# The opening stage of a two-layer hybrid decoder trunk: the scaled x in PSUM, and scalar operands in place of one-column tensors

## The chip, the cores and the metric

The kernel runs on one core of a Trainium2 chip. The metric is device time in microseconds (us) for one execution; the figure for a kernel is the median of its runs. A profile is one more execution, taken with the hardware profiler; its span goes from the first instruction to the last.

The engines are named as in the profile: PE is TensorE (matrix products; PEld is its weight load), DVE is VectorE, ACT is ScalarE, POOL is GpSimd and SP is SyncE, which here issues DMA transfers. SBUF is the on-chip memory for tiles, PSUM the smaller one (eight banks) into which PE writes its products. DVE and ACT can read and write both.

## The reference

x has 512 positions of width 1024, c is one conditioning vector of width 1024, and there are two layers:

```python
sc = jax.nn.silu(c)
for layer in range(DEPTH):
    ...
    mod = sc @ w_mod[layer] + b_mod[layer]
    shift1, scale1, gate1, shift2, scale2, gate2 = [m[:, None, :] for m in jnp.split(mod, 6, axis=-1)]

    h = rmsnorm(x, g_attn[layer]) * (1.0 + scale1) + shift1
    o = mixer_layer(h, w_in[layer], w_out[layer], diff_lambda[layer], subln_g[layer],
                    forget_bias[layer], lam_init, cos_a, sin_a, cos_b, sin_b)
    x = x + gate1 * o

    h = rmsnorm(x, g_mlp[layer]) * (1.0 + scale2) + shift2
    up = h @ w_up[layer]
    ...
    x = x + gate2 * ((jax.nn.silu(g) * u) @ w_down[layer])
return rmsnorm(x, g_final)
```

`mixer_layer` is one input projection, three kinds of attention heads and an output projection. The change touches only how the first h of layer 0 is made: the columns of `mod` for shift1 and scale1, and the line that forms h.

## The kernel before

**Layout.** x lies transposed in SBUF, as eight tiles k of 128 features by 512 positions. Every float32 operand of a large product is split in two: a rounded part hi (hh, whi) and the rest lo (hl, wlo). A product is then three matmuls, hi by hi, lo by hi and hi by lo (lines L251, L252, L253). A weight tile is loaded by DMA into raww, rounded by ACT (L174), and the rest is formed by DVE (L186).

**The opening stage (first 52 us).** c is spread over the partitions by a small product and passed through SiLU; the result stays in two PSUM tiles, cps, of 512 columns each, and also in SBUF as scb. The weight rows of w_mod for shift1 and scale1 come in as sixteen transfers of 512 KB: mu[m] holds, for the 128 features of column m, the rows of scale1 (j = 1) and of shift1 (j = 0). While they arrive, the squares of x are summed by PE into ps0, and rstd, the reciprocal root of the mean square, is made from it by ACT (L288, L289) in a PSUM tile.

Then, for each column m from 0 to 7, `unit(m)` computes the two entries of `mod`, and `attn_init` forms h and multiplies it by the first q and k weights. An entry is a dot product of a row of mu with scb. It is made in one of two ways:

- on DVE, as two products with running sum (L1043, halves of 512, mu from SBUF and cps from PSUM);
- on POOL, for the eight columns of the list POOL_COLS (shift1 of columns 1 to 7, and scale1 of column 6): POOL multiplies mu by scb (L1036, both in SBUF), ACT sums the products (L1037), and DVE adds the bias bm (L1038).

After scale1 of column m, DVE forms `scl = (1 + scale1) * g_attn` (L1046). `h_part` then does three things: DVE writes ht = x * scl * rstd (L297); ACT writes hh, which is ht + shift1 rounded (L299); DVE writes hl = (ht + shift1) - hh (L300). PE then does six matmuls, three each for q and k (L251 to L253, into the PSUM tiles qkps). After column 7 come the split of the V weights (L174, L186) and the V projection (L404 to L406), then the attention of layer 0.

**Order and buffers.** The program is written as one sequence; a planner then sets the order on each engine, places semaphores, and gives tiles their buffers. Each engine works through its own list in order. A tile pool has a fixed number of buffers for each tag, and a new tile waits until an old one is released by its last reader. ht comes from the pool tp (SBUF, tag "e", four buffers). The PSUM banks are divided into mm (three), ps_s (two), ps_t with tag "pt" (two) and ps_o (one). In the opening, the two cps hold two of the mm banks until the last L1043, ps0 holds one pt bank until rstd is formed, qkps hold both ps_s banks, and rstd holds ps_o until the last L297. The first V projection takes its four PSUM tiles from ps_o, ps_t, mm and ps_t.

`h_part` also serves all later norms (with halves of 256 columns), from other callers; those call it without the new argument.

Of the kernel before, what the change touches and what calls it, by code (L numbers as in the profile page):

```python
# [8 lines left out]
F32 = mybir.dt.float32  # L9
F32R = mybir.dt.float32r  # L10
AF = mybir.ActivationFunctionType
ALU = mybir.AluOpType
AX = mybir.AxisListType

SEQ = 512
# [15 lines left out]
def kernel(  # L31
# [27 lines left out]
    V, A, T, G = nc.vector, nc.scalar, nc.tensor, nc.gpsimd  # L59
# [10 lines left out]
    mm = ctx.enter_context(tc.tile_pool(name="mm", bufs=3, space=PS))  # L70
    ps_s = ctx.enter_context(tc.tile_pool(name="ps_s", bufs=2, space=PS))
    ps_t = ctx.enter_context(tc.tile_pool(name="ps_t", bufs=2, space=PS))
    ps_o = ctx.enter_context(tc.tile_pool(name="ps_o", bufs=1, space=PS))

    def tmp(name, tag):
        if tag == "rp":
            return rpp[0].tile([128, SEQ], F32, tag=tag, name=name, bufs=4)
        return tp.tile([128, SEQ], F32, tag=tag, name=name, bufs=4)
# [6 lines left out]
    def tick():  # L85
        for g in list(aux):
            if next(g, StopIteration) is StopIteration:
                aux.remove(g)
# [13 lines left out]
    gA = const.tile([128, DEPTH, KC], F32, name="gA")  # L102
# [8 lines left out]
    modc = const.tile([128, DEPTH, 48], F32, name="modc")  # L111
    scl = const.tile([128, DEPTH, 2, KC], F32, name="scl")
# [156 lines left out]
    ALL = slice(0, SEQ)  # L269
# [18 lines left out]
            A.activation(out=r[:, c], in_=ps[:, c], func=AF.Ln, bias=eps[:, 0:1], scale=1.0 / DM)  # L288
        A.activation(out=r[:, c], in_=r[:, c], func=AF.Exp, scale=-0.5)  # L289

    def h_part(h, l, which, k, r, c=ALL):
        if len(h) == k:
            h.append(pair_tiles(hs, "hs", "h"))
        hi, lo = h[k]
        t = tmp("ht", "e")
        sh = modc[:, l, 24 * which + k:24 * which + k + 1]
        V.scalar_tensor_tensor(out=t[:, c], in0=x[:, k, c], scalar=scl[:, l, which, k:k + 1], in1=r[:, c],  # L297
                               op0=ALU.mult, op1=ALU.mult)
        anchor[1] = A.activation(out=hi[:, c], in_=t[:, c], func=AF.Identity, bias=sh, scale=1.0).ins  # L299
        anchor[0] = V.scalar_tensor_tensor(out=lo[:, c], in0=t[:, c], scalar=sh, in1=hi[:, c].bitcast(F32),  # L300
                                           op0=ALU.add, op1=ALU.subtract).ins
# [22 lines left out]
    def attn_init(l, unit=None, ps0=None, nst=None):  # L324
        st = Init()
        h, r = nst or ([], ps_o.tile([128, SEQ], F32, tag="o", name="rstd"))
        st.h = h
        n0 = len(h)
        st.qps = [ps_s.tile([128, SEQ], F32, tag="s", name="qkps") for _ in range(2)]
        ws = []  # L330

        def q_part(k, c):
            first, last = k == 0, k == KC - 1
            for j in range(2):
                mm3(st.qps[j], ws[j](128 * k, 128 * k + 128), h[k], first, last, c)

        for half, c in enumerate(HALVES if unit is None else (ALL,)):
            if half or nst is None:
                rstd_part(r, c, ps0)
            for k in range(KC):  # L340
                if unit is not None:
                    unit(k)
                if half or k >= n0:
                    h_part(h, l, 0, k, r, c)
                if not ws:
                    ws += [W.use() for _ in range(2)]
                q_part(k, c)
                if half == 1 and k in (1, 3, 5):
                    W.pump(k // 2)
        return st  # L350
# [633 lines left out]
    with ExitStack():  # L984
        V.memset(ones, 1.0)
        V.memset(eps[:, 0:1], 1e-6)
        V.memset(eps[:, 1:2], 1e-5)
        for t, a in ((bm, bmod), (gA, gattn)):
            G.dma_start(out=t, in_=a)
        ropes = ExitStack()  # L990
        ropep[0] = ropes.enter_context(tc.tile_pool(name="rope0", bufs=1))
        with tc.tile_pool(name="start", bufs=1) as stp:
            W.pt = stp
            scp = []
            crow = [tmp("crow", "e") for _ in range(2)]
            for q in range(2):
                nc.sync.dma_start(out=crow[q][0:1, :], in_=cT[:, 512 * q:512 * q + 512])
            for q in range(2):
                cps = mm.tile([128, SEQ], F32, tag="mm", name="cps")
                T.matmul(cps, ones[0:1, :], crow[q][0:1, :], start=True, stop=True)  # L1000
                A.activation(out=scb[:, 512 * q:512 * q + 512], in_=cps, func=AF.Silu)
                last_silu[0] = A.activation(out=cps, in_=cps, func=AF.Silu).ins
                scp.append(cps)
            mus = {}
            last_load = [None]
            def mu_load(u):
                mus[u] = stp.tile([128, 2, 1024], F32, tag="mu", name="mu", bufs=6)
                for j in (1, 0):
                    src = wmod[0, 8 * j + u]
                    last_load[0] = nc.sync.dma_start(out=mus[u][:, j, :], in_=src).ins  # L1010

            for op in STARTUP:
                if op[0] == "m":
                    mu_load(int(op[1]))
                elif op == "w":
                    W.dma(W.nd + 1)
                else:
                    k = int(op[1])
                    nc.sync.dma_start(out=x[:, k:k + 2, :], in_=xT[:, k:k + 2, :])
            ps0 = ps_t.tile([128, SEQ], F32, tag="pt", name="ssps")  # L1020
            for k in range(KC):
                sq = tmp("sq", "ev")
                A.activation(out=sq, in_=x[:, k, :], func=AF.Square)
                if k % 2 == 0:
                    sq0 = sq
                    continue
                V.tensor_tensor(out=sq, in0=sq, in1=sq0, op=ALU.add)
                T.matmul(ps0, ones, sq, start=(k == 1), stop=(k == KC - 1))
            W.lo(2)

            def unit(m):
                for j in (1, 0):
                    ci = 8 * j + m
                    mu, dst, bias = mus[m][:, j, :], modc[:, 0, ci:ci + 1], bm[:, 0, ci:ci + 1]
                    if (m, j) in POOL_COLS:
                        G.tensor_tensor(out=mu, in0=mu, in1=scb, op=ALU.mult)  # L1036
                        A.activation(out=mu, in_=mu, func=AF.Copy, accum_out=dst)  # L1037
                        V.tensor_tensor(out=dst, in0=dst, in1=bias, op=ALU.add)  # L1038
                    else:
                        mp = sm.tile([128, 1], F32, tag="mp", name="mp")  # L1040
                        for q in range(2):
                            mq = mu[:, 512 * q:512 * q + 512]
                            V.tensor_tensor_reduce(out=mq, in0=mq, in1=scp[q], scale=1.0, scalar=mp if q else bias,  # L1043
                                                   op0=ALU.mult, op1=ALU.add, accum_out=dst if q else mp)
                    if j == 1:
                        V.scalar_tensor_tensor(out=scl[:, 0, 0, m:m + 1], in0=modc[:, 0, ci:ci + 1], scalar=1.0,  # L1046
                                               in1=gA[:, 0, m:m + 1], op0=ALU.add, op1=ALU.mult)

            rt0 = load_rope(ORDER[0][0])
            st = attn_init(0, unit, ps0)  # L1050
            W.pt = None
            with tc.issue_after(last_load[0]):
                for t, a in ((fb, fbias), (cst, consts), (sg, sublng), (gM, gmlp), (gF, gfin), (cw, convw),
                             (cb, convb)):
                    nc.sync.dma_start(out=t, in_=a)
        for l in range(DEPTH):
            if l:
                ropep[0] = ropes.enter_context(tc.tile_pool(name="rope%d" % l, bufs=1))
            with ropes, tc.tile_pool(name="attn%d" % l, bufs=8) as ap:
                rpp[0] = ap  # L1060
                W.pt = ap
                if l:
                    st = attn_init(l, nst=nst)
                    rt0 = load_rope(ORDER[0][0])
                nst = layer_attn(l, ap, [(0, u) for u in range(16, 40)] if l == 0 else [], st, rt0)
            with tc.tile_pool(name="mlp%d" % l, bufs=34) as mp:
                while any(g.__name__ == "mod_gen" for g in aux):
                    tick()
                anchor[0] = gate[0]
                if l == 0:  # L1070
                    aux.append(mod_gen([(0, u) for u in range(40, 48)] + [(1, u) for u in range(48)], 200))
                nst = layer_mlp(l, mp, nst)
                while aux:
                    tick()
# [106 lines left out]
```

## Time and profile before

| | us |
|---|---|
| median of three runs | 1338.02 |
| lowest and highest of them | 1337.93, 1339.64 |
| the profiled execution | 1334.63 |
| its span | 1332.9 |
| busy: PE, DVE, ACT, POOL | 1277.8, 858.2, 642.3, 22.9 |

The mean granted clock of PE is 0.989 of full speed over the span. The profile has a page of totals and shares, and views that can be asked for one stretch: what each engine waited for (a row names the waiting engine and line, the releasing one, the sum of the waits in us, how many, and the longest), instructions in order of time (start, duration, engine, line, what it writes and reads; in brackets the idle time before it), groups of instructions of one line and shape (count, sum of busy time in us and mean in ns, then the idle time before them and who ended it), and tables of busy time by stretch. Almost all of POOL's 22.9 us lies in the first 38 us.

### The profile page before, as it was taken

How to read it: one execution, taken by the hardware profiler on the slowest of the kernel's cores; microseconds unless marked ns; L12 is line 12 of the kernel's file. 1: busy time of each engine (PE TensorE's matmuls, PEld its weight loads, DVE VectorE, ACT ScalarE, POOL GpSimd, SP SyncE). 2: the span in 40 equal slices, each digit the busy share in tenths (PEclk: the TensorE clock that was granted, in tenths of full speed). 3: DMA queues.
4: the chain of work that ended last, by engine and by line, in shares of the span. 5: the costliest groups of instructions: out<-in, count | busy, mean ns of one | idle time of the engine just before them, and what ended most of it. 6: DMA issues, size and time to landing. Idle time of an engine off the chain costs nothing.

```text
span 1332.9 us, 17722 instructions
## 1 busy us (share of the span) xinstructions
PE 1277.8 (96%) x6568; PEld 1058.6 (79%) x6568; DVE 858.2 (64%) x1600; ACT 642.3 (48%) x1158; POOL 22.9 (2%) x16
## 2 busy tenths in 40 slices
PE   4899999999999999999999999999999999999997
PEld 1788888788877778888898888878878888888886
DVE  6888999868888874423347788875754444443232
ACT  5576677745333243322336677785543333333231
POOL 5100000000000000000000000000000000000000
PEclk8899999999999999999999999999999999999999
DMA  9345454433888853332432334212133333332331
GB/s 373 140 141 183 152 180 136 130 110 129 269 261 266 267 173 95 91 103 87 117 110 95 90 103 141 66 56 90 48 109 96 97 95 95 95 91 87 103 99 63
DMA packets 56601, 174.39 MB, mean 131 GB/s; under 512 B 8130, under 2 KB 10450, under 8 KB 56516
## 3 DMA queue, kind: packets, MB, share of 16 engines
q1 hardware_dynamic: 55364, 172.16, 41.0%
q8 instruction: 52, 0.85, 0.3%
q10 hardware_dynamic: 1088, 1.05, 0.2%
q14 instruction: 33, 0.27, 0.1%
q0 software_dynamic: 64, 0.06, 0.0%
HBM read 159.41 MB, written 2.10 MB: 121 GB/s over the span
## 4 chain that ended last, share of the span: by engine, by line
PE 53%; DMA 8%; DVE 7%; ACT 4%; issue 3%; SPq 0%; DVEq 0%; ACTq 0%
DMA rawm<-in_wmod_dram 7%; PE dps L251 6%; PE dps L253 6%; PE dps L252 6%; PE pu L251 4%; PE pu L253 4%; PE pu L252 4%; PE pg L252 4%; PE pg L253 4%; PE pg L251 4%; DVE wlo L186 1%; DVE rawm L217 1%; PE qkps L251 1%; PE qkps L252 1%; PE qkps L253 1%
## 5 line engine op out<-in xcount | busy, mean ns | idle before, releaser
L186 DVE TENSOR_TENSOR wlo<-raww,whi 128x1024 fp32r<-128x1024 f32 (+3 forms) x188 | 224.2, 1193 | 241.0 <-ACT whi L174 236.5
L174 ACT ACTIVATE whi<-raww 128x1024 fp32r<-128x1024 f32 (+3 forms) x188 | 194.5, 1035 | 329.6 <-PE dps L252 137.7
L253 PE MATMUL pu<-hh,wlo 128*128 128x512 f32 (+1 forms) x368 | 141.2, 384 | 3.5 <-DVE wlo L186 3.5
L252 PE MATMUL pg<-hl,whi 128*128 128x512 f32 (+1 forms) x368 | 143.0, 389 | 1.5 <-DVE hl L300 1.5
L251 PE MATMUL pg<-hh,whi 128*128 128x512 f32 (+1 forms) x368 | 141.6, 385 | 1.6 <-ACT whi L174 1.6
L251 PE MATMUL pu<-hh,whi 128*128 128x512 f32 (+1 forms) x368 | 142.4, 387 | 0.5 <-ACT whi L174 0.5
L253 PE MATMUL pg<-hh,wlo 128*128 128x512 f32 (+1 forms) x368 | 140.9, 383 | 1.1 <-DVE wlo L186 1.1
L252 PE MATMUL pu<-hl,whi 128*128 128x512 f32 (+1 forms) x368 | 140.7, 382 | 0.0
L251 PE MATMUL dps<-mh,whi 128*128 128x512 f32 x308 | 121.5, 395 | 0.0
L253 PE MATMUL dps<-mh,wlo 128*128 128x512 f32 x308 | 121.5, 394 | 0.0
L252 PE MATMUL dps<-ml,whi 128*128 128x512 f32 x308 | 121.2, 393 | 0.0
L217 DVE CUSTOM_DVE_ANT_0 rawm<-rawm,scb,bm 128x1024 f32<-128x1024 f32 x80 | 102.3, 1279 | 23.7 <-DMA rawm<-in_wmod_dram 23.4
L654 ACT ACTIVATE e<-e,nm 128x256 f32<-128x256 f32 (+3 forms) x160 | 89.0, 557 | 33.0 <-DVE nm L641 29.9
L251 PE MATMUL qkps<-hh,whi 128*128 128x512 f32 x224 | 95.1, 424 | 4.7 <-ACT qk L434 4.1
L898 ACT ACTIVATE y<-y 128x512 f32<-128x512 f32 x44 | 27.8, 632 | 142.6 <-DVE y L895 142.6
L252 PE MATMUL qkps<-hl,whi 128*128 128x512 f32 x224 | 89.7, 400 | 0.0
L253 PE MATMUL qkps<-hh,wlo 128*128 128x512 f32 x224 | 89.6, 400 | 0.0
L253 PEld LDWEIGHTS pu<-hh,wlo 128*128 128x128 f32 x368 | 69.1, 188 | 22.1 <-DVE wlo L186 6.9
L641 DVE CUSTOM_DVE_ANT_0 e<-s,cst 128x256 f32<-128x256 f32 (+3 forms) x160 | 76.4, 481 | 12.0 <-PE s L628 3.7
L252 PEld LDWEIGHTS pg<-hl,whi 128*128 128x128 f32 x368 | 69.0, 188 | 17.7 <-DVE hl L300 3.1
L253 PEld LDWEIGHTS pg<-hh,wlo 128*128 128x128 f32 x368 | 69.0, 188 | 16.7 <-DVE wlo L186 1.9
L251 PEld LDWEIGHTS pg<-hh,whi 128*128 128x128 f32 x368 | 69.1, 188 | 16.0 <-ACT whi L174 2.0
(176 smaller groups left out, 2663.2 us busy)
## 6 DMA issues: line engine op xcount, KB each, us to landing
raww<-in_wup_dram SPq DMA_DIRECT2D x88, 512.0 KB
rawm<-in_wmod_dram SPq DMA_DIRECT2D x80, 512.0 KB
raww<-in_wqk_dram SPq DMA_DIRECT2D x32, 512.0 KB
raww<-in_wdown_dram SPq DMA_DIRECT2D x32, 512.0 KB
mu<-in_wmod_dram SPq DMA_DIRECT2D x16, 512.0 KB
raww<-in_wout_dram SPq DMA_DIRECT2D x16, 448.0 KB
raww<-in_wv_dram SPq DMA_DIRECT2D x12, 512.0 KB
raww<-in_wdown_dram SPq DMA_DIRECT2D x16, 384.0 KB
```

Source lines behind the costliest of these rows:

```text
L174: A.activation(out=h[:, 0:m], in_=self.raw[i][:, c:c + m], func=AF.Copy)
L186: V.tensor_tensor(out=lo[:, 0:m], in0=raw[:, c:c + m], in1=h[:, 0:m].bitcast(F32), op=ALU.subtract)
L217: V.tensor_tensor_reduce(out=raw, in0=raw, in1=scb, scale=1.0, scalar=bm[:, l, ci:ci + 1], op0=ALU.mult, op1=ALU.add, accum_out=dst)
L251: T.matmul(ps[:, c], w[0], rhs[0][:, c], start=first, stop=False, skip_group_check=True)
L252: T.matmul(ps[:, c], w[0], rhs[1][:, c], start=False, stop=False, skip_group_check=True)
L253: T.matmul(ps[:, c], w[1], rhs[0][:, c], start=False, stop=last, skip_group_check=True)
L641: anchor[0] = V.tensor_tensor_reduce(out=e[:, 0:n], in0=s[:, 0:n], in1=cst[:, mask + SEQ - n:mask + SEQ], scale=-scale, scalar=3e38, op0=A ...
L654: anchor[1] = A.activation(out=e[:, 0:n], in_=e[:, 0:n], func=AF.Exp, bias=nm, scale=-1.0, accum_out=den).ins
L898: last_silu[0] = A.activation(out=y, in_=y, func=AF.Silu).ins
```

## The change

Three edits, all in the opening of layer 0. ht is written to PSUM there, in an mm bank for even k and a pt bank for odd k. The addition of the bias to a column summed by ACT (L1038) becomes a tensor_scalar whose scalar is read per partition. The same is done with the formation of scl (L1046).

```diff
-    def h_part(h, l, which, k, r, c=ALL):
+    def h_part(h, l, which, k, r, c=ALL, ps=False):
...
-        t = tmp("ht", "e")
+        t = (mm, ps_t)[k % 2].tile([128, SEQ], F32, tag=("mm", "pt")[k % 2], name="ht") if ps else tmp("ht", "e")
...
-                    h_part(h, l, 0, k, r, c)
+                    h_part(h, l, 0, k, r, c, ps=unit is not None)
...
-                        V.tensor_tensor(out=dst, in0=dst, in1=bias, op=ALU.add)
+                        V.tensor_scalar(out=dst, in0=dst, scalar1=bias, scalar2=None, op0=ALU.add)
...
-                        V.scalar_tensor_tensor(out=scl[:, 0, 0, m:m + 1], in0=modc[:, 0, ci:ci + 1], scalar=1.0,
-                                               in1=gA[:, 0, m:m + 1], op0=ALU.add, op1=ALU.mult)
+                        V.tensor_scalar(out=scl[:, 0, 0, m:m + 1], in0=modc[:, 0, ci:ci + 1], scalar1=1.0,
+                                        scalar2=gA[:, 0, m:m + 1], op0=ALU.add, op1=ALU.mult)
```

`unit` is given only in the opening of layer 0, so `ps` is true only there. The dot products, the shift, the splits and the matmuls are the same as before, and no transfer is added or removed.

## The prediction, made before the changed kernel was run

> **What bounds the kernel now.** I read the page first (busy time by engine, the chain that ended last), then what TensorE (PE) waited for in the whole run, longest first.
>
> ```profile
> PE 1277.8 (96%) x6568; PEld 1058.6 (79%) x6568; DVE 858.2 (64%) x1600; ACT 642.3 (48%) x1158; POOL 22.9 (2%) x16
> PE 53%; DMA 8%; DVE 7%; ACT 4%; issue 3%; SPq 0%; DVEq 0%; ACTq 0%
> ```
> ```profile
> PE ssps L1028 <- DVE sq L1027: 8.6, 1, 8.6
> PE qkps L251 <- ACT hh L299: 6.6, 3, 4.8
> PE qkps L252 <- DVE hl L300: 6.3, 3, 2.6
> PE qkps L251 <- ACT qk L434: 4.1, 2, 2.1
> PE pu L253 <- DVE wlo L186: 3.5, 7, 0.8
> ```
>
> PE is busy 96% of the span and leads the chain, so a change pays only if PE starts its work earlier or idles less. Its largest idle sums, rows one to three, are all in the opening stage, where h is made (L297 to L300) and the first q and k columns are multiplied (L251 to L253); L300 and L299 are lines that the change touches. Behind the opening no sum is above 4.1 us. Next the stretches of the opening; the columns are stretch, its length, busy time (and instructions) of PE, weight loads, DVE, ACT, POOL, then PE's granted clock, DMA share and GB/s.
>
> ```profile
> 23.00:52.24 29.24, 18.60 (x49) 12.05 (x49) 27.93 (x51) 14.71 (x24) 15.32 (x7) 0.65 0.52 200
> 33.19:36.61 3.42, 2.98 (x7) 2.16 (x7) 3.42 (x8) 1.76 (x3) 3.42 (x2) 0.52 1.05 402
> 36.61:40.02 3.41, 1.42 (x5) 0.67 (x4) 3.41 (x6) 0.00 (x0) 1.71 (x2) 0.99 0.31 80
> 40.02:43.43 3.41, 2.55 (x6) 1.97 (x7) 3.37 (x12) 2.89 (x5) 0.00 (x0) 0.50 0.01 2
> 43.43:46.85 3.42, 3.42 (x8) 2.21 (x8) 3.35 (x8) 2.75 (x6) 0.00 (x0) 0.52 0.00 0
> 46.85:50.26 3.41, 2.74 (x12) 1.88 (x10) 2.57 (x8) 1.92 (x4) 0.00 (x0) 1.00 0.00 0
> 52.00:64.00 12.00, 12.00 (x99) 11.94 (x98) 7.54 (x12) 4.22 (x7) 0.00 (x0) 1.00 0.55 205
> ```
>
> From 23.00 to 52.24 DVE is busy 27.93 of 29.24 us: **DVE bounds the opening**. From 52.24, when the V projection starts, PE is busy without a gap. The DMA share falls to 0.31 in the third row and to nothing after it, so the opening's loads are in by about 38 us and do not set its end. The timelines of DVE, POOL and PE (start, us, what) show where DVE's time goes.
>
> ```profile
> 25.97 2.52 DVE L300 SCALAR_TENSOR_TENSOR hl<-ht,modc,hh 128x512 fp32r<-128x512 f32 x1
> 28.41 2.32 DVE L1046 SCALAR_TENSOR_TENSOR scl<-modc,gA 128x1 f32<-128x1 f32 x1
> ...
> 31.39 2.17 DVE L300 SCALAR_TENSOR_TENSOR hl<-ht,modc,hh 128x512 fp32r<-128x512 f32 x1
> 33.49 0.74 DVE L297 SCALAR_TENSOR_TENSOR ht<-x,scl,rstd 128x512 f32<-128x512 f32 x1
> 34.15 0.74 DVE L1043 CUSTOM_DVE_ANT_0 mu<-mu,cps,mp 128x512 f32<-128x512 f32 x1
> 34.81 0.08 DVE L1043 DVE_READ_ACCUMULATOR2_ANT modc<- 128x1 f32 x1
> 34.81 1.01 DVE L1038 TENSOR_TENSOR modc<-modc,bm 128x1 f32<-128x1 f32 x1
> ...
> 36.41 2.26 DVE L300 SCALAR_TENSOR_TENSOR hl<-ht,modc,hh 128x512 fp32r<-128x512 f32 x1
> 38.60 0.15 DVE L1046 SCALAR_TENSOR_TENSOR scl<-modc,gA 128x1 f32<-128x1 f32 x1
> ...
> 50.41 0.75 DVE L300 SCALAR_TENSOR_TENSOR hl<-ht,modc,hh 128x512 fp32r<-128x512 f32 x1 [0.79 <-ACT hh L299]
> ```
> ```profile
> 19.48 18.65 POOL L1036 TENSOR_TENSOR mu<-mu,scb 128x1024 f32<-128x1024 f32 x7 [7.83 <-DMA mu<-in_wmod_dram]
> ```
>
> The same L300 takes 2.17 to 2.52 us while POOL multiplies (19.48 to 38.07 us) and 0.75 us afterwards; the 128x1 operations take 2.32 and 1.01 us in place of 0.15. What suffers has its tensor inputs in SBUF. What has one of two in PSUM does not: L297 (rstd in PSUM) and L1043 (cps in PSUM) keep 0.74 us at 33.49 and 34.15, in the midst of POOL's work. The wait hangs on two inputs from SBUF.
>
> **The change, part by part.** *ht in PSUM.* L300 then reads one tensor from PSUM, as L297 and L1043 do. Three of the eight L300 fall in POOL's time: 2.52 + 2.17 + 2.26 - 3 x 0.75 = 4.70 us less. *L1046 and L1038 as tensor_scalar.* One of each waits inside DVE's busy stretch: 2.32 - 0.15 = 2.17 and 1.01 - 0.15 = 0.86, together 3.03 us. Sum on DVE: **7.73 us**. (The two weight splits of L186 at 18.89 us, also slow, stay as they are.) The prices of the new forms, from the groups by line and shape:
>
> ```profile
> L312 DVE SCALAR_TENSOR_TENSOR x<-dps,modc,x 128x512 f32<-128x512 f32 x14 | 10.5, 750 | 30.6 <-PE dps L253 30.6
> L669 DVE SCALAR_TENSOR_TENSOR e<-e,rd 128x512 f32<-128x512 f32 x8 | 6.0, 746 | 0.1
> L356 DVE TENSOR_SCALAR sg<-sg 128x1 f32<-128x1 f32 x2 | 0.3, 146 | 0.0
> L1001 ACT ACTIVATE scb<-cps 128x512 f32<-128x512 f32 x2 | 1.2, 597 | 3.0 <-PE cps L1000 3.0
> L1002 ACT ACTIVATE cps<-cps 128x512 f32<-128x512 f32 x2 | 1.2, 592 | 0.0
> ```
>
> A PSUM input costs DVE 750 against 746 ns, a tensor_scalar 146 ns against 0.15 us. No row shows DVE writing PSUM; ACT writes PSUM in 592 against 597 ns to SBUF. By these rows eight ht tiles cost between -0.04 and +0.03 us: nothing. L299 reading PSUM on ACT is priced the same way, and ACT has slack (14.71 of 29.24 us).
>
> *Waits added.* Two of the three mm banks hold cps until the last L1043, so the even ht share one bank: ht of column k+2 must wait for L300 of column k. In DVE's own order it stands behind that L300 already (ht of column 2, at 33.49, behind L300 of columns 0 and 1), so this costs nothing; without that order it would be one L300, 0.75 us, per even column, with DVE's column products behind it. The odd ht alternate between two pt banks once rstd is computed. The V projection's banks now wait for the last ht, but its first matmul stands on PE behind the L252 of column 7, which needs the same L300: nothing added. The change adds no DMA, and no instruction passes a queue.
>
> *What is late next.* Taking DVE's order as it is, without the waits, an L300 ends where it ended less the waits ahead of it and its own: column 0 at 26.7 us (25.97 + 0.75), column 1 at 28.2 (31.39 + 0.75 - 1.77 - 2.17), column 2 at 31.0 (less 1.42 and 0.86 more), column 7 at 43.4 (50.41 + 0.75 - 7.73). ACT, half idle, keeps up with its hh and its sums of POOL's products, and POOL still ends by 38 us, ahead of column 7. PE may not keep up, because of its clock:
>
> ```profile
> 45.23 0.63 PE L253 MATMUL qkps<-hh,wv 128*128 128x512 f32 x1
> 45.66 0.63 PE L252 MATMUL qkps<-hl,wv 128*128 128x512 f32 x1
> ...
> 47.33 0.40 PE L253 MATMUL qkps<-hh,wv 128*128 128x512 f32 x1
> 47.56 0.40 PE L252 MATMUL qkps<-hl,wv 128*128 128x512 f32 x1
> ```
>
> Start to start a matmul takes 0.43 us at granted clock 0.5 and 0.23 at 1.0. At half clock throughout, the 46 matmuls behind the first L300 take 46 x 0.43 = 19.8 us from 26.7: PE ends at 46.5 in place of 52.24, a gain of 5.7. At full clock for the last columns DVE sets the end and the gain is 7.7. The clock rows say which is nearer: it rose after a stretch in which PE was busy 2.98 of 3.42 us, and again after 3.42 of 3.42; it fell after 1.42 of 3.41. In the new order the first three columns keep PE at work from 26.7 us for (18 - 2) x 0.43 = 6.9 us, to 33.6, without a gap (each L300 above is early enough), twice such a stretch, so the rise comes before column 4. I take **7.2 us**, half a microsecond below the upper end for a possible fall of the clock between the later columns. Nothing behind 52.24 starts at a fixed time, so the whole gain reaches the end. Against the profiled execution (1334.63 us, span 1332.9) that is 1327.4 us. The median of the three runs is 1338.02, 3.4 us above it; I predict against the median: 1338.02 - 7.2 = **1330.8 us**.
>
> *The skill against the second edit.* The rows above show waits only for two SBUF tensors. The Trainium skill (SBUF — State Buffer, Who interferes with whom) counts tensor_scalar among the operations that can enter a two-port mode and then take the same port pair as GpSimd. [...]
>
> **The rivals.** *PE at half clock throughout* (worked out above): gain 5.7, 1332.3 us. Against it speaks the rise after busy stretches; for it, that the clock stayed at 0.50 through 40.02 to 43.43 with PE busy 2.55 of 3.41.
>
> *The small operations still wait.* L300 gains its 4.70, but tensor_scalar waits for POOL as the old forms did. With DVE ahead, some five of them in separate places fall before 38 us; at half a POOL product each (18.65/7/2 = 1.3 us, and some overlap) they take about 5.5 us in place of 3.03: gain 2.2, 1335.8 us. For it: no row excludes it. Against: the one tensor input of such an operation leaves nothing for a second read.
>
> *The change doesn't do what it says*: L300 waits with ht in PSUM too. Gain at most the 3.03 us of the small ones, 1335.0, and more likely under 2, about 1337. L297 and L1043 speak against it.
>
> *Slower: the order behind the opening.* The order on each engine is planned from costs; new operands in the opening can turn choices in layer 0's attention, where DVE is nearly full. The price is that of a wait which is there now:
>
> ```profile
> 140.00:150.00 10.00, 7.89 (x38) 6.82 (x38) 8.62 (x23) 5.89 (x16) 0.00 (x0) 0.83 0.38 106
> ```
>
> PE idles 10.00 - 7.89 = 2.1 us, on a q or k split (L434, longest wait 2.1 us above), and a mean clock of 0.83 over 10 us is 3.4 us at half clock, which cost 1.7 us of work: 3.8 us together. One new such wait leaves a gain of 3.4, two make it nothing (1338.4), three give 1330.8 + 11.4 = **1342.2 us**: from the third on this decides. Against it: no instruction behind the opening changes.
>
> **How the numbers follow.** Forecast (1329.5 to 1332) 0.67; half clock 0.14; small operations still waiting 0.08, half of it within 0.2%; no effect on L300 0.03; new waits behind the opening 0.08, half with two (no change), half with three. About 0.2% (2.7 us) is what a measurement here can tell from no change. Faster 0.67 + 0.14 + 0.04 = 0.85, same 0.04 + 0.03 + 0.04 = 0.11, slower 0.04. The range reaches up to the small operations' rival, 1336, and down to the upper end of the gain with the 3.4 us by which the profiled execution lay under the median: 1338.02 - 7.73 - 3.4, about 1327.
>
> **What would show it.** Right: every L300 near 0.75 us while POOL works; L1046 and L1038 near 0.15; DVE through L300 of column 7 by about 43.5 us and the V projection's first matmul (L404) at 44.5 to 46.5; every later stage as long as before. Half clock: PE without gaps from 27 us and clock 0.5 until 46. Small operations waiting: L1046 or L1038 above 1 us before 38 us. Order: the V projection early, but new PE waits between 64 and 310 us. I am wrong if L300 stays above 2 us, or if L404 starts early and the end does not move.

## The result and the profile after

The changed kernel's median is 1330.86 us (eight runs, 1328.54 to 1334.49) against 1338.2 us for the kernel before (eight runs, 1335.56 to 1339.64): 7.3 us less. The ratio is 0.9947, with a 95% interval of 0.9932 to 0.9962. The profiled execution took 1329.34 us, its span 1327.6 us, 5.3 us less than the span before. Among the experiments below, one run of the kernel before (1418.61 us) and one of e8 (2506.64 us) lie far outside the rest, and the ratios leave them out.

The page's busy times of the changed kernel, and then what PE waited for, show what changed as a whole:

```profile
PE 1276.8 (96%) x6568; PEld 1057.6 (80%) x6568; DVE 849.8 (64%) x1600; ACT 642.6 (48%) x1158; POOL 22.1 (2%) x16
```
```profile
PE ssps L1028 <- DVE sq L1027: 8.9, 1, 8.9
PE qkps L251 <- ACT hh L299: 6.5, 4, 5.5
...
PE qkps L252 <- DVE hl L300: 1.8, 2, 1.0
```

DVE has the same 1600 instructions and is busy 8.4 us less (858.2 before). PE's wait for L300 fell from 6.3 to 1.8 us; the first wait for x's squares stayed. The instructions of DVE and POOL in the opening, in order of time:

```profile
26.22 0.74 DVE L300 SCALAR_TENSOR_TENSOR hl<-ht,modc,hh 128x512 fp32r<-128x512 f32 x1
26.88 0.20 DVE L1046 TENSOR_SCALAR scl<-modc,gA 128x1 f32<-128x1 f32 x1
27.00 0.20 DVE L1038 TENSOR_SCALAR modc<-modc,bm 128x1 f32<-128x1 f32 x1
...
43.18 0.75 DVE L300 SCALAR_TENSOR_TENSOR hl<-ht,modc,hh 128x512 fp32r<-128x512 f32 x1 [0.76 <-ACT hh L299]
```
```profile
19.76 17.87 POOL L1036 TENSOR_TENSOR mu<-mu,scb 128x1024 f32<-128x1024 f32 x7 [7.86 <-DMA mu<-in_wmod_dram]
```

POOL multiplies from 19.8 to 37.6 us (19.5 to 38.1 before), and none of these operations of DVE takes longer beside it. The groups of DVE's instructions between 19.7 and 37.6 us (count, busy time, mean ns of one) say it for all of them:

```profile
L186 DVE TENSOR_TENSOR wv<-raww,wv 128x1024 fp32r<-128x1024 f32 x2 | 4.5, 2295 | 0.3 <-ACT wv L174 0.3
...
L300 DVE SCALAR_TENSOR_TENSOR hl<-ht,modc,hh 128x512 fp32r<-128x512 f32 x5 | 3.7, 745 | 0.2 <-ACT hh L299 0.2
...
L1038 DVE TENSOR_SCALAR modc<-modc,bm 128x1 f32<-128x1 f32 x4 | 0.8, 207 | 0.0
L1046 DVE TENSOR_SCALAR scl<-modc,gA 128x1 f32<-128x1 f32 x4 | 0.8, 204 | 0.0
```

Five L300 beside POOL take 745 ns each, where three took 2.17 to 2.52 us. Only L186, which the change leaves with two SBUF tensors, still takes 2.3 us each. The stretches of the opening (PE, weight loads, DVE, ACT, POOL, then granted clock, DMA share, GB/s) and the first matmul of the V projection:

```profile
23.00:45.02 22.02, 16.27 (x48) 10.25 (x49) 20.79 (x51) 14.53 (x24) 14.83 (x7) 0.84 0.70 269
...
25.10:31.90 6.80, 6.11 (x14) 4.32 (x15) 6.65 (x18) 4.99 (x9) 6.80 (x4) 0.50 1.02 408
31.90:45.02 13.12, 10.17 (x36) 5.93 (x35) 12.04 (x30) 9.46 (x15) 5.93 (x4) 1.00 0.47 174
```
```profile
45.02 0.64 PE L404 MATMUL vps<-whi,hh 128*128 128x262 f32 x4
```

The V projection starts at 45.02 us in place of 52.24, 7.22 us earlier. DVE is still the busiest engine there: it is busy for 20.79 of 22.02 us, against 27.93 of 29.24 before, so its busy time fell by 7.14 us and its idle time by 0.08. PE ran at half clock from 25.1 to 31.9 us only, and at full clock after it.

### The profile page after: what moved, and what is told of

The parts are those of the page before. It is cut to its first block, busy times and chain, and to the rows that moved or that the text cites. A ratio compares the mean times of both kernels' runs of the same rounds, so it can differ in the third digit from the quotient of the medians.

```text
span 1327.6 us, 17720 instructions
## 1 busy us (share of the span) xinstructions
PE 1276.8 (96%) x6568; PEld 1057.6 (80%) x6568; DVE 849.8 (64%) x1600; ACT 642.6 (48%) x1158; POOL 22.1 (2%) x16
## 4 chain that ended last, share of the span: by engine, by line
PE 55%; DMA 7%; DVE 7%; ACT 4%; issue 3%; SPq 0%; DVEq 0%; ACTq 0%
DMA rawm<-in_wmod_dram 7%; PE dps L251 6%; PE dps L253 6%; PE dps L252 6%; PE pu L251 4%; PE pu L253 4%; PE pu L252 4%; PE pg L252 4%; PE pg L253 4%; PE pg L251 4%; PE qkps L251 1%; PE qkps L252 1%; PE qkps L253 1%; DVE rawm L217 1%; DVE wlo L186 1%
## 5 line engine op out<-in xcount | busy, mean ns | idle before, releaser
L186 DVE TENSOR_TENSOR wlo<-raww,whi 128x1024 fp32r<-128x1024 f32 (+3 forms) x188 | 224.4, 1194 | 240.9 <-ACT whi L174 236.4
```

What stands on the lines that cost most here:

```text
L186: V.tensor_tensor(out=lo[:, 0:m], in0=raw[:, c:c + m], in1=h[:, 0:m].bitcast(F32), op=ALU.subtract)
```

## The experiments

The theory: a DVE operation waits for POOL's products when it reads two tensors from SBUF, the change takes away such pairs, and DVE's shorter list of work brings the V projection forward. The rivals: the new order on DVE did it; the scalar edits are worth nothing; L300 was slow for a reason other than POOL; something else than DVE sets the opening's end.

Each experiment was profiled, and all but e6 were timed against the kernel before on the same chip. The start of the V projection (L404) is the sharper measure, since single runs of one kernel lie up to 9.4 us apart (the kernel before: 1330.38 to 1339.75 us beside e1, e2 and e5), while L404 came at 45.02 and 44.92 us in two profiles of the changed kernel.

| kernel | L404, us | median, us | kernel before there, us | ratio, 95% interval |
|---|---|---|---|---|
| e1, ht in PSUM alone | 49.61 | 1333.9 | 1336.29 | 0.9983, 0.9971 to 0.9995 |
| e2, scalars alone | 50.10 | 1334.31 | 1336.29 | 0.9987, 0.9974 to 0.9999 |
| e5, rstd to SBUF | 50.12 | 1333.56 | 1336.29 | 0.9984, 0.9971 to 0.9998 |
| e3, before without POOL | 49.65 | 1335.47 | 1337.72 | 0.9979, 0.9965 to 0.9993 |
| e4, changed without POOL | 49.56 | 1333.61 | 1337.72 | 0.9975, 0.9961 to 0.9989 |
| e7, squares first | 44.35 | 1329.51 | 1337.72 | 0.9932, 0.9908 to 0.9957 |
| e8, x before mu[1] too | 42.06 | 1326.8 | 1337.22 | 0.9916, 0.9896 to 0.9937 |
| e9, as e8, seven POOL columns | 42.62 | 1327.63 | 1337.22 | 0.9925, 0.9903 to 0.9948 |
| e10, changed kernel again | 44.92 | 1330.01 | 1337.22 | 0.9941, 0.9921 to 0.9961 |

### One part of the change at a time

e1 is the changed kernel with the two small operations put back:

```diff
-                        V.tensor_scalar(out=dst, in0=dst, scalar1=bias, scalar2=None, op0=ALU.add)
+                        V.tensor_tensor(out=dst, in0=dst, in1=bias, op=ALU.add)
...
-                        V.tensor_scalar(out=scl[:, 0, 0, m:m + 1], in0=modc[:, 0, ci:ci + 1], scalar1=1.0,
-                                        scalar2=gA[:, 0, m:m + 1], op0=ALU.add, op1=ALU.mult)
+                        V.scalar_tensor_tensor(out=scl[:, 0, 0, m:m + 1], in0=modc[:, 0, ci:ci + 1], scalar=1.0,
+                                               in1=gA[:, 0, m:m + 1], op0=ALU.add, op1=ALU.mult)
```

> ht in PSUM, but L1038 and L1046 as in the kernel before. Theory (a DVE operation with two SBUF tensors waits for POOL's products): every L300 near 0.75 us, L1038 and L1046 still wait 1 us or more in places before 38 us; the V projection (L404) starts at 47.5 to 50 us, between the 45.0 of the changed kernel and the 52.2 of the kernel before; time 2 to 5 us under the kernel before. Rival (the gain comes from the new order on DVE, not from shorter operations): DVE's order is here that of the kernel before but for one swap, so L404 stays near 52 us. Rival (tensor_scalar is worth nothing): L404 at 45 us, as in the changed kernel.

e2 is the kernel before with only the opposite of this diff, ht staying in SBUF.

> L1038 and L1046 as tensor_scalar, ht in SBUF as before. Theory: L1038 and L1046 at 0.2 us throughout; the L300 that fall before 38 us still take 2 us or more, and as DVE is ahead there may be one more of them; L404 at 49 to 52 us, time 0 to 3 us under the kernel before. Rival (the order): L404 near 45 us, since the order on DVE is here nearly that of the changed kernel.

DVE's instructions in e1, in order of time:

```profile
26.34 0.74 DVE L300 SCALAR_TENSOR_TENSOR hl<-ht,modc,hh 128x512 fp32r<-128x512 f32 x1
27.00 1.33 DVE L1046 SCALAR_TENSOR_TENSOR scl<-modc,gA 128x1 f32<-128x1 f32 x1
28.26 0.15 DVE L1038 TENSOR_TENSOR modc<-modc,bm 128x1 f32<-128x1 f32 x1
29.00 0.74 DVE L300 SCALAR_TENSOR_TENSOR hl<-ht,modc,hh 128x512 fp32r<-128x512 f32 x1
30.98 2.04 DVE L1038 TENSOR_TENSOR modc<-modc,bm 128x1 f32<-128x1 f32 x1
33.61 0.74 DVE L300 SCALAR_TENSOR_TENSOR hl<-ht,modc,hh 128x512 fp32r<-128x512 f32 x1
34.27 1.07 DVE L1046 SCALAR_TENSOR_TENSOR scl<-modc,gA 128x1 f32<-128x1 f32 x1
36.59 1.06 DVE L1046 SCALAR_TENSOR_TENSOR scl<-modc,gA 128x1 f32<-128x1 f32 x1
```

The groups of e2's DVE instructions between 19.5 and 38.6 us:

```profile
L300 DVE SCALAR_TENSOR_TENSOR hl<-ht,modc,hh 128x512 fp32r<-128x512 f32 x4 | 8.0, 2008 | 0.0
...
L1038 DVE TENSOR_SCALAR modc<-modc,bm 128x1 f32<-128x1 f32 x3 | 0.6, 201 | 0.0
L1046 DVE TENSOR_SCALAR scl<-modc,gA 128x1 f32<-128x1 f32 x3 | 0.6, 200 | 0.0
```

Each edit frees its own operations and no others. In e1 all L300 are short while four small operations wait; in e2 four L300 wait, one more than before, while the small ones are short. L404 comes 2.63 us earlier in e1 and 2.14 us in e2, and both times lie 2 us under the kernel before. The order as the cause falls by e1: its order on DVE is that of the kernel before but for one swap, and L404 still comes 2.63 us earlier. e2 does not test it as expected: its order on DVE is not close to that of the changed kernel. Of its 49 DVE instructions from the first L1043 behind the weight split to the last L300, 38 can be matched in sequence with the changed kernel's, no more than for the kernel before. What speaks on the order in the full change is the sum above: almost all of the 7.22 us is shorter busy time, not closed gaps. The order still decides which operations meet POOL. That tensor_scalar is worth nothing falls too.

The two gains make 4.77 us, but together the edits gave 7.22. The reason is in the rows: the operations that still wait take over part of what the others saved. In e1 the small ones lose 1.33 + 2.04 + 1.07 + 1.06 - 4 x 0.15 = 4.9 us, where they lost 3.03 in the kernel before. In e2 the four L300 lose 8.03 - 4 x 0.75 = 5.03 us, where three lost 4.70. A DVE that is ahead meets POOL more often, until no operation of either kind is left that can wait.

### The wait goes where the SBUF pair goes

e5 is the changed kernel with rstd of the opening in SBUF, so that L297 reads two tensors from SBUF and L300 one:

```diff
-        h, r = nst or ([], ps_o.tile([128, SEQ], F32, tag="o", name="rstd"))
+        h, r = nst or ([], tmp("rstd", "e"))
```

> The changed kernel with rstd of the opening in SBUF in place of PSUM, so that L297 has two SBUF tensors and L300 one. Theory: the wait changes places: L297 before 38 us takes 2 us or more where it took 0.75, L300 stays at 0.75; four or five L297 with 1.2 to 1.7 us each put L404 at 49 to 52 us. Rival (L300 was slow for another reason, such as its fp32r output): L297 stays at 0.75 us and L404 at 45 us.

The groups of e5's DVE instructions between 19.7 and 39.3 us:

```profile
L297 DVE SCALAR_TENSOR_TENSOR ht<-x,scl,rstd 128x512 f32<-128x512 f32 x5 | 8.7, 1749 | 0.0
...
L300 DVE SCALAR_TENSOR_TENSOR hl<-ht,modc,hh 128x512 fp32r<-128x512 f32 x4 | 3.0, 740 | 0.0
```

L297, untouched in arithmetic, shape and output, now takes 1749 ns on the mean of five (four of them 1.28 to 2.86 us), L300 stays at 740, and L404 falls back to 50.12 us. The four long L297 are together 5.0 us above 0.75 us each, and L404 is 5.10 us later than in the changed kernel; the order on DVE, which is that of e2, need not be called on to explain it. So it is the place of the input tensors, not the line, its output type or PSUM as such. POOL is slower too where DVE has more such operations: its seven products took 17.87 us in the changed kernel, 18.65 in the kernel before and 19.63 in e5.

### Without POOL there is nothing to gain

e3 is the kernel before and e4 the changed kernel, both with all sixteen columns on DVE:

```diff
-POOL_COLS = [(int(u[0]), int(u[1])) for u in "10 20 30 40 50 60 70 61".split()]
+POOL_COLS = []
```

> The kernel before with the list POOL_COLS empty: all sixteen columns are summed on DVE (L1043), POOL multiplies nothing. Theory: without POOL nothing waits: every L300 near 0.75 us, L1046 near 0.15 us, the two L186 at 19 us near 1.2 us each in place of 2.3. DVE saves 7.7 + 2.1 us and has 8 columns of 1.33 us more, one of them in its idle time at 10 us: L404 at 51 to 53 us. Rival (L300 waits for something else than POOL): L300 above 2 us again.

> The changed kernel with POOL_COLS empty. Theory: without POOL the edits have nothing to remove, so L404 starts within 0.7 us of where it starts in the kernel before with the same list, and the two times agree within 0.2%. Rival (the edits help by themselves, through PSUM or through the order): L404 some us earlier than there.

DVE's instructions of e3, the old forms with no POOL beside them:

```profile
17.11 2.50 DVE L186 TENSOR_TENSOR wv<-raww,wv 128x1024 fp32r<-128x1024 f32 x2 [0.28 <-ACT wv L174]
22.19 0.75 DVE L300 SCALAR_TENSOR_TENSOR hl<-ht,modc,hh 128x512 fp32r<-128x512 f32 x1
...
31.64 0.75 DVE L300 SCALAR_TENSOR_TENSOR hl<-ht,modc,hh 128x512 fp32r<-128x512 f32 x1
```

Every L300 of e3 takes 0.75 us with ht in SBUF, and the two L186 take 2.50 us together in place of 4.51. L404 stands at 49.65 us in e3 and 49.56 in e4: without POOL the edits are worth 0.1 us, and the two ratios lie on each other. (L404 came earlier than the 51 to 53 us expected, because with no sum of POOL's products ahead of the squares on ACT, rstd also was done 2 us earlier.) A by-product: in the kernel before, POOL's help was worth less than the waits that it caused, since L404 is 2.6 us earlier without POOL; in the changed kernel POOL brings it 4.5 us forward.

### Which DVE operations wait

e6 adds two operations per column to the changed kernel, behind L1046:

```diff
+                        for n in (256, 255):
+                            V.tensor_scalar(out=mu[:, 0:n], in0=x[:, m, 0:n], scalar1=2.0, scalar2=None, op0=ALU.mult)
```

> The changed kernel with two more operations per column: tensor_scalar of 256 and of 255 elements from x in SBUF into a used part of mu in SBUF; their results are used by nothing. Theory (only a second SBUF tensor waits for POOL): all sixteen take under 0.5 us, beside POOL too. Rival (a tensor_scalar of many elements also takes the port that POOL uses): those before 38 us take 1 us or more, the later ones under 0.5. The total time is of no interest here.

In order of time (POOL's products end at 37.7 us here):

```profile
27.06 1.35 DVE L1049 TENSOR_SCALAR mu<-x 128x256 f32<-128x256 f32 x1
29.00 1.82 DVE L1049 TENSOR_SCALAR mu<-x 128x255 f32<-128x255 f32 x1
33.76 1.76 DVE L1049 TENSOR_SCALAR mu<-x 128x256 f32<-128x256 f32 x1
36.10 1.98 DVE L1049 TENSOR_SCALAR mu<-x 128x255 f32<-128x255 f32 x1
40.11 0.28 DVE L1049 TENSOR_SCALAR mu<-x 128x256 f32<-128x256 f32 x1
```

Here the theory in its plain form falls: these read one tensor, and beside POOL they take 1.35 to 1.98 us in place of 0.28. So two SBUF tensors are one way to wait, and a longer tensor_scalar from SBUF to SBUF is another. The tensor_scalar of the second edit does not wait: L1046 and L1038, 128x1, stay at 0.20 to 0.21 us beside POOL in every run that has them as tensor_scalar. They differ from those of e6 in having a single element per partition, and also in reading their scalar per partition where e6 has a constant. No run separates the two; that the single element is what counts is argued.

### What sets the opening's end now

e7 to e9 ask for what limits the changed kernel. e7 puts ACT's sums of POOL's products behind the squares of x:

```diff
-                A.activation(out=sq, in_=x[:, k, :], func=AF.Square)
+                last_sq = A.activation(out=sq, in_=x[:, k, :], func=AF.Square).ins
...
-                        A.activation(out=mu, in_=mu, func=AF.Copy, accum_out=dst)
+                        with tc.issue_after(last_sq): A.activation(out=mu, in_=mu, func=AF.Copy, accum_out=dst)
```

> The changed kernel, with ACT's sums of POOL's products (L1037) placed behind the squares of x. In the changed kernel the first L1037 stands ahead of the squares on ACT and waits for POOL until 12 us while x is already there. Theory (DVE sets the opening's end, and starts its columns when rstd and the first weight split are done): the squares start at about 9 us, rstd is done 3 to 4 us earlier, the two L186 run before POOL's long stretch and take 2.4 us together in place of 4.5; L404 at 41 to 43 us, time 2 to 4 us under the changed kernel. Rival (the loads of mu, the last of them landing at about 32 us, or POOL, which ends at 38 us, set the end): L404 stays within 1 us of 45.

The squares started at 10.6 us in place of 13.0, but rstd was done only 1.2 us earlier (3 to 4 were expected), the second L186 still ran into POOL (3.19 us), and L404 moved by 0.7 us to 44.35. That is within the 1 us of the rival, but it does not show that loads or POOL set the end. The condition that the theory named, L186 ahead of POOL, was not met. e8 meets it, by the order of the loads:

```diff
-STARTUP = "m0 m1 x0 x2 x4 x6 w w m2 m3 m4 m5 m6 m7 w w".split()
+STARTUP = "m0 x0 x2 x4 x6 w w m1 m2 m3 m4 m5 m6 m7 w w".split()
```

> As e7, and the loads of x and of the first two weights moved ahead of mu[1] in the opening. Theory (after the change DVE still sets the end, and starts its columns late because rstd and the weight split L186, itself slowed by POOL, come first): squares at 6 to 9 us, both L186 done before POOL's long stretch (2.4 us together), the first L297 at 15 to 18 us; then the last product of POOL, near 37.5 us as before, is what is late: ACT sum 1.25, L1038 0.2, L299 0.7, L300 0.75 and the last four matmuls about 1 us put L404 at 41 to 42.5 us, time 2 to 4 us under the changed kernel on the same chip. Rival (the loads set the end): L404 stays at 44 to 45 us.

e9 takes column 6's scale1 ("61") off POOL's list as well:

> As e8, with scale1 of column 6 summed on DVE, so that POOL has seven products. If POOL's last product sets the end in e8, it ends 2.4 us earlier here and DVE, with 1.33 us more work, has room: L404 1 to 2 us earlier than in e8. If DVE sets the end there, L404 is 1 to 1.5 us later than in e8.

DVE's instructions of e8, then its stretch from the first L297 to the V projection:

```profile
14.82 2.36 DVE L186 TENSOR_TENSOR wv<-raww,wv 128x1024 fp32r<-128x1024 f32 x2 [0.26 <-ACT wv L174]
...
18.21 0.76 DVE L297 SCALAR_TENSOR_TENSOR ht<-x,scl,rstd 128x512 f32<-128x512 f32 x1 [0.37 <-ACT rstd L289]
...
40.22 0.75 DVE L300 SCALAR_TENSOR_TENSOR hl<-ht,modc,hh 128x512 fp32r<-128x512 f32 x1 [0.75 <-ACT hh L299]
```
```profile
18.20:42.06 23.86, 15.99 (x49) 8.83 (x49) 21.84 (x54) 15.56 (x26) 17.99 (x9) 0.93 0.84 329
```

The two L186 take 2.36 us, the first L297 stands at 18.21 us in place of 24.24, and L404 at 42.06. So loads do not hold it at 45. Of the 6 us of earlier start half is left: the two products of column 1's scale1 now come behind that start, and DVE idles 2.0 of the 23.86 us in place of 1.2 of 22.02, at L300 mostly for ACT's hh. Taking work from POOL (e9) made L404 0.56 us later and not earlier, which speaks against POOL's last product as what sets the end in e8 and for DVE. But DVE had 1.33 us more work there, so it had room for more than half of it in e8: neither of the two expected results came, and what sets the end of e8 stays partly open. e8 beats both kernels in its median, 1326.8 us against 1330.01 for the changed kernel and 1337.22 for the kernel before on the same chip; its interval overlaps that of the changed kernel, so of the step from there the trace is the better witness.

### Where 2 us went again

The profiled span fell by 5.3 us, though L404 came 7.22 us earlier. The changed kernel once more:

> The changed kernel once more, on the same chip as e8 and e9, to compare with. The opening repeats: L404 at 45.0 us within 0.3. If the 2 us that the first profile of it lost again between 45 and 108 us belong to the window of half clock at 83 us, which depends on when short idle times of PE fall, then this profile shows the loss only where its clock rows show such a window there; if they belong to the new order, the loss is there in every profile.

Two stretches can be laid side by side: from L404 to the first product of the forget bias (pf, L537), and from there to the first split of a finished pair of heads (L242). The kernel before, the changed kernel, its repeat e10, and e4:

```profile
52.24:86.80 34.56, 34.18 (x234) 31.17 (x233) 26.79 (x66) 19.98 (x41) 0.00 (x0) 1.00 0.50 172
86.80:108.20 21.40, 21.07 (x130) 18.03 (x130) 19.31 (x52) 15.23 (x34) 0.00 (x0) 1.00 0.56 185
```
```profile
45.02:80.50 35.48, 34.54 (x234) 31.22 (x233) 26.76 (x66) 20.15 (x41) 0.00 (x0) 1.00 0.51 167
80.50:102.90 22.40, 22.26 (x130) 19.25 (x130) 19.26 (x52) 15.24 (x34) 0.00 (x0) 0.92 0.55 178
```
```profile
44.92:80.40 35.48, 34.54 (x235) 31.27 (x233) 26.85 (x66) 20.14 (x41) 0.00 (x0) 1.00 0.52 167
80.40:104.40 24.00, 23.85 (x130) 20.76 (x130) 19.21 (x52) 15.22 (x34) 0.00 (x0) 0.86 0.51 167
```
```profile
49.56:85.30 35.74, 35.17 (x234) 31.89 (x232) 26.15 (x65) 20.08 (x40) 0.00 (x0) 0.97 0.42 133
85.30:106.70 21.40, 21.07 (x129) 18.02 (x129) 19.30 (x51) 15.21 (x34) 0.00 (x0) 1.00 0.56 185
```

The first stretch is 0.92 us longer in the changed kernel, and again in e10: at full clock, so this belongs to the program and not to the clock. PE idles 0.94 us there in place of 0.38; the largest part is a new wait for DVE's L706:

```profile
78.30 0.39 PE L729 MATMUL po<-ptl,vv 128*128 128x256 f32 x1 [0.56 <-DVE ptl L706]
```

The order on PE, DVE and ACT differs between the two programs up to about 64 us in the changed kernel (72 in the kernel before) and is the same behind that. That the order makes the loss, and not the earlier start, is argued, not shown. The second stretch goes with the clock: 21.4 us at 1.00, 22.4 at 0.92, 24.0 at 0.86, whichever the program; the other traces agree, with about 22.5 us at 0.92 in e1, e2, e3, e5 and e8 and about 24 at 0.86 in e7. Half clock lasted from about 83 to 86.4 us in the changed kernel and from 81.3 to 88.1 in e10. e10 and the changed kernel are one program, and they differ by 1.6 us there. So the 0.9 us comes with the new program, most likely from its order, and the rest is a stretch of half clock that falls differently from execution to execution.

## Why the prediction was right

**The bound, the mechanism and the time.** That DVE sets the opening's end, and that a second SBUF tensor makes it wait for POOL, is what e5 and e3 show. L404 at 45.02 lies within the 44.5 to 46.5 us named, 7.22 us ahead where 7.2 was taken, and the median fell by 7.3.

**The sum on DVE.** From the first L1043 behind the weight split to the last L300 DVE took 27.09 us before (23.32 to 50.41) and 19.61 after (23.57 to 43.18): 7.48 us less, against 7.73. That L404 moved by 7.22, so near to the 7.2 forecast, is in part luck: the 7.2 was 7.73 less half a microsecond for a fall of the clock. The clock did not fall. The half went elsewhere, 0.25 us in the sum and 0.25 because the columns began that much later (23.57 in place of 23.32). Two details of the sum were off. tensor_scalar was priced at 146 ns from a row whose scalar is a constant; with a scalar read per partition it takes 204 to 207 ns, and 0.12 us from start to start (26.88 to 27.00) where the old L1046, at 38.60 before, was followed after 0.07. And 4.70 and 3.03 are not what each edit gives by itself (2.63 and 2.14 for L404): the terms of the sum hold only together.

**PE's clock.** The rise was expected before column 4; it came at 31.9 us, in column 2. Half clock throughout did not occur, and a fall between the later columns did not either, though PE was busy 10.17 of 13.12 us.

**No added wait.** One mm bank for the even ht cost nothing: DVE's longest idle time at an L300 is the 0.76 us ahead of the last one, for ACT's hh, where it was 0.79 in the kernel before, and at the L297, which write ht, no idle time is listed.

**The small operations.** The prediction left open whether tensor_scalar still waits. In the 128x1 form used here it does not. The reason that the prediction gave for this, that the one tensor input leaves nothing for a second read, is wrong: e6's operations have one tensor input too, and wait. The Trainium skill (SBUF — State Buffer, Who interferes with whom) was right to count tensor_scalar among the operations that can take the port, as e6 shows at 255 and 256 elements (1.35 to 1.98 us against 0.28). For one element, the Trainium skill's Advanced Engine Details and Errata, Mode Summary, with its odd count above one, agrees with the 0.20 us. The condition in the Trainium skill's Vector Engine (DVE) Microarchitecture Reference, Performance modes, is put on a non-unit dimension, which a single element does not have; read so, it agrees too.

**The step that was wrong in part.** "Nothing behind 52.24 starts at a fixed time, so the whole gain reaches the end", and, against the last rival, that no instruction behind the opening changes. No instruction did, but their order did, up to about 64 us, and the stretch from L404 to the forget bias became 0.9 us longer: the last rival in small. The profiled pair lost another 1.0 us to a stretch of half clock. That the median shows the full gain all the same is luck, since single runs scatter by more than that: the agreement of 7.3 with 7.2 is closer than these runs can vouch for, as the interval of the ratio (0.9932 to 0.9962, or 5 to 9 us) says.

## What to carry to other kernels

When an operation of DVE takes two or three times its usual time only while GpSimd works, look at where its operands lie: moving one of two SBUF tensors to a free PSUM bank, or replacing a one-column tensor by a per-partition scalar, takes the wait away at hardly any price. Do it for every operation in that stretch, since those that are left take over part of the wait. And don't count on tensor_scalar as such: with 255 or 256 elements from SBUF to SBUF it waited as well. And when a stage is shortened by a few microseconds, check whether the planned order behind it is still the same.

## What the runs showed of the hardware that was not expected

- A tensor_scalar of 255 or 256 elements with one SBUF tensor and a constant waits for GpSimd's products (1.35 to 1.98 us against 0.28); one of a single element with its scalar read per partition does not (0.20).
- A 128x1 tensor_scalar with a scalar read per partition took 204 to 207 ns, one with a constant 146 ns.
- Some 3.4 us of half clock in the attention of layer 0 cost 1.0 us, and 6.8 us of it 2.6 us, against the same stretch at full clock; how much of it comes differs between two executions of one program. Runs of one kernel scatter by 6 to 9 us.
